# Rotary embedding on one core: the two tables brought in 8 rows of 8 KB instead of 16 of 4 KB, in the place of slabs 4-5, and no early write of zeros

## The chip, the cores and the metric

The kernel runs on one core of a Trainium2 chip. The metric is the device time of one execution in microseconds. A profile comes from one further execution on the same chip: its *span* runs from the first to the last instruction, and its own time lies a little above the span. TensorE is PE, VectorE DVE, ScalarE ACT, GpSimd POOL; SyncE (SP) computes nothing here and issues DMAs. A core has 16 DMA engines, and an issue on SP's or ACT's queue is spread over them.

## The reference

`x` is (16, 512, 1024) in float32, 16 heads of 64; `cos` and `sin` are (512, 32). Each half of a head is rotated by the angle of its position:

```python
x = x.reshape(batch, seq, num_heads, head_dim)
x1, x2 = x[..., :half_dim], x[..., half_dim:]
cos = cos[None, :, None, :]
sin = sin[None, :, None, :]
rotated = np.concatenate([x1 * cos - x2 * sin,
                          x1 * sin + x2 * cos], axis=-1)
```

So 33.55 MB are read and 33.55 MB written; the tables are 64 KB each.

## The kernel before, in words

**Slabs and places.** The 16 batches form four pairs of *slabs*, 8 MB a pair. A pair covers four batches; each of the 128 partitions holds 16 successive positions of it, the first 8 in the even slab, the other 8 in the odd one, so that a slab has 4 MB, 8192 numbers (32 KB) on each partition. There are three *places* in SBUF, each for two slabs (64 KB on each partition). Slabs 0-1 and 6-7 use place 0, slabs 2-3 place 1, slabs 4-5 place 2. A slab is worked on in its own place: the cast to bf16, the products and the cast back to float32 all lie there.

**Order of the DMAs.** Loads and stores of slabs all go through `issue` (line 66), on SP's queue, and keep the order of the program: load 0, load 1, load 2-3 (even partitions, then odd ones), load 4-5 (whole), then store 0-1 in two halves, load 6-7 in two halves, store 2-3, store 4-5 in halves, store 6-7. An instruction of SP that has to wait holds up all issues behind it. A store waits for ACT's last cast of its slabs, load 6-7 for store 0-1 to have left place 0.

**Tables.** A partition needs cos and sin of its own 8 positions: those of the even slabs in `tabs[0]`, of the odd ones in `tabs[1]`. Each table is read in 16 rows (`TP`) of 1024 numbers (`TW`, 4 KB), one row on every 8th partition (`TS`), by ACT's queue (line 91), into a tile that DVE has set to zero before (line 90). DVE casts both to bf16 (`tab1`, line 114). PE then spreads the rows over all 128 partitions: `pick` holds matrices of 0 and 1 (or −1, for the sign of sin in the lower half), made by POOL (lines 103 to 107), and a matmul with such a matrix copies row j to the partitions it belongs to. A row of 4 KB covers 32 positions and so serves two neighbouring partitions; the index `e` (0 or 1) tells which of the two, and two masked matmuls are added in PSUM (line 122), 16 matmuls in all. DVE copies the first result to bf16 (line 129), ACT the second (through line 154).

**The zeros.** A tile `blank` of 1 x 128 is set to zero (line 84), and ACT's queue writes its 512 bytes to the start of the output (line 93) right behind the tables. Store 0-1 later overwrites them.

**The passes.** For each slab ACT casts x to bf16 (into the first half of the slab's own bytes), DVE multiplies it by the sin and cos tables (line 170, two products), adds the two (line 173) with the halves of a head exchanged, and ACT casts the sum back to float32. ACT casts slab s+1 before it casts slab s back. Slab 0 is done in two passes of 4 positions, slab 7 in three (4, 2, 2).

Of the kernel before, what the change touches and what calls it, by code (L numbers as in the profile page):

```python
# [2 lines left out]

# [4 lines left out]


@with_exitstack  # L10
def kernel(
    ctx: ExitStack,
    tc: tile.TileContext,
    x: bass.AP,
    cos: bass.AP,
    sin: bass.AP,
    num_heads: int,
    out: bass.AP,
):
    nc = tc.nc  # L20
    P = nc.NUM_PARTITIONS

    batch, seq, dim = x.shape
    nh = num_heads
    hd = dim // nh
    half = hd // 2
    bf16 = mybir.dt.bfloat16
    f32 = mybir.dt.float32

    nb = 2  # L30
    nslabs = batch // nb
    rpp = nb * seq // P
    W = rpp * dim
    TP = 16
    TS = P // TP
    TW = seq * half // TP

    out_flat = out.rearrange("b s h d -> b s (h d)")

    singles = ctx.enter_context(tc.tile_pool(name="singles", bufs=1))  # L40
    pairs = ctx.enter_context(tc.tile_pool(name="pairs", bufs=3))
    psum = ctx.enter_context(tc.tile_pool(
        name="psum", bufs=1, space=bass.MemoryType.PSUM))


    def view(t, offset, *dims):
        return dataclasses.replace(t, offset=t.offset + offset,
                                   ap=[t.ap[0], *[list(d) for d in dims]])

    places = [pairs.tile([P, 2 * W], f32, tag="pair", name="pair") for _ in range(3)]


    def here(s, n=1):
        return view(places[s // 2 % 3], s % 2 * W, (1, n * W))


    def there(t, s, n=1):  # L60
        return bass.AP(tensor=t.tensor, offset=t.offset + s // 2 * 2 * P * W + s % 2 * W,
                       ap=[[2 * W, P], [1, n * W]])


    def issue(out, in_):
        tc.keep_in_program_order(nc.sync.dma_start(out=out, in_=in_))  # L66


    def load(s, n=1, parts=slice(None)):
        issue(here(s, n)[parts], there(x, s, n)[parts])  # L70


    def store(s, n=1, parts=slice(None)):
        issue(there(out_flat, s, n)[parts], here(s, n)[parts])


    EVEN, ODD = slice(0, P, 2), slice(1, P, 2)


    load(0)  # L80


    blank = singles.tile([1, P], f32, tag="blank")
    nc.vector.memset(blank, 0.0)  # L84


    cos_sb = singles.tile([P, TW], f32, tag="cos_sb")
    sin_sb = singles.tile([P, TW], f32, tag="sin_sb")
    for t, src in ((cos_sb, cos), (sin_sb, sin)):
        nc.vector.memset(t, 0.0)  # L90
        tc.keep_in_program_order(nc.scalar.dma_start(out=t[::TS], in_=bass.AP(
            tensor=src.tensor, offset=src.offset, ap=[[TW, TP], [1, TW]])))
    tc.keep_in_program_order(nc.scalar.dma_start(out=bass.AP(
        tensor=out_flat.tensor, offset=out_flat.offset, ap=[[P, 1], [1, P]]), in_=blank))

    load(1)
    for parts in (EVEN, ODD):
        load(2, 2, parts)
    load(4, 2)


    pick = singles.tile([P, 4 * P], bf16, tag="pick")
    nc.gpsimd.memset(pick, 0.0)  # L103
    for e in range(2):
        for g in range(2):
            part = view(pick, (2 * e + g) * P + e, (2 * TP, P // (2 * TP)), (2, TP))
            nc.gpsimd.affine_select(  # L107
                out=part, in_=part, compare_op=mybir.AluOpType.not_equal,
                fill=1.0 - 2.0 * g, base=0, pattern=[[0, P // (2 * TP)], [-TS, TP]],
                channel_multiplier=1)  # L110

    tab1 = singles.tile([P, 2 * TW], bf16, tag="tab1")
    for i, t in enumerate((cos_sb, sin_sb)):
        nc.vector.tensor_copy(out=view(tab1, i * TW, (1, TW)), in_=t)  # L114

    accs, tabs = [], []
    for h in range(2):
        acc = psum.tile([P, 2 * rpp * hd], f32, tag=f"acc{h}", name="acc")
        for i in range(2):
            for f in range(2):  # L120
                for e in range(2):
                    nc.tensor.matmul(  # L122
                        view(acc, i * rpp * hd + f * half, (hd, rpp), (1, half)),
                        view(pick, (2 * e + i * f) * P, (1, P)),
                        view(tab1, i * TW + (2 * e + h) * rpp * half, (half, rpp), (1, half)),
                        start=e == 0, stop=e == 1)
        accs.append(acc)
        tabs.append(singles.tile([P, 2 * rpp * hd], bf16, tag=f"tab{h}", name="tab"))
    nc.vector.tensor_copy(out=tabs[0], in_=accs[0])  # L129

    passes = []
    for s in range(nslabs):
        r = 0
        for n in {0: (4, 4), nslabs - 1: (4, 2, 2)}.get(s, (rpp,)):
            passes.append((s, r, n))
            r += n


    def halves(u):
        s, r, n = u
        t = here(s).bitcast(bf16)
        return [view(t, (2 * r + i * n) * dim, (1, n * dim)) for i in range(2)]


    def cast(u):
        s, r, n = u
        copy(halves(u)[0], view(here(s), r * dim, (1, n * dim)))  # L150


    def copy(out, in_):
        tc.keep_in_program_order(nc.scalar.copy(out=out, in_=in_))  # L154


    for i, u in enumerate(passes):
        s, r, n = u
        if i == 0:
            cast(u)  # L160
            cast(passes[1])
            copy(tabs[1], accs[1])
            cast(passes[2])
        elif s > 0:
            for v in passes:
                if v[0] == s + 1:
                    cast(v)
        lo, up = halves(u)
        for t, a in ((up, 0), (lo, rpp * hd)):
            nc.vector.tensor_mul(  # L170
                out=t, in0=lo,
                in1=view(tabs[s % 2], a + r * hd, (hd, n), (0, nh), (1, hd)))
        nc.vector.tensor_add(  # L173
            out=up, in0=up, in1=view(lo, half, (hd, n * nh), (-half, 2), (1, half)))

        copy(view(here(s), r * dim, (1, n * dim)), up)
        if s == 1:
            for act in (store, load):
                for parts in (EVEN, ODD):
                    act(0 if act is store else 6, 2, parts)  # L180
        elif s % 2 and r + n == rpp:
            for parts in (EVEN, ODD) if s == 5 else (slice(None),):
                store(s - 1, 2, parts)


# [1 line left out]
_INS = ['x', 'cos', 'sin', 'num_heads']  # L187
_OUTS = [((16, 512, 16, 64), 'float32')]

_NUMBERS = {'num_heads': 16}  # L190


# [26 lines left out]
```

## Time and profile before

| | |
|---|---|
| median of 3 runs | 162.04 us (161.72 to 162.29) |
| the profiled execution | 162.13 us, span 160.3 us |
| read / written over the span | 33.69 MB / 33.55 MB, 419 GB/s |
| casts of 8192 columns on ACT | 7.02 us each, 12 of them |
| products and sums of 8192 columns on DVE | 4.42 us each, 18 of them |
| matmuls (all for the tables) | 16, 3.7 us busy |
| memset of one table tile | 0.91 us |
| cos and sin, from issue to landing | 7.5 and 9.1 us |

A line of the timeline gives the start in us, the length, the engine, the line of the kernel, the operation with output and input, and how many were merged; in brackets the idle time before it and what ended that. "SPq" and "ACTq" are the issues of DMAs on these queues. In a table of windows the columns are the stretch, its length, each engine's busy time with the number of instructions, the granted clock, the busy share of the DMA engines and their rate. DMA packets are recorded one by one with start, duration, bytes and queue, though not with the engine that moved them; q1 is SP's queue and q10 ACT's. A packet counts in the window in which it starts, so that in windows of a few us the share can be read as above 1.

### The profile page before, as it was taken

The numbers are of one execution on the slowest core, as the hardware profiler recorded it, in microseconds if no ns is written. First come the engines' busy times: TensorE is split into PE (matmuls) and PEld (weight loads), VectorE is DVE, ScalarE is ACT, GpSimd is POOL, SyncE is SP. The second block draws the span as 40 slices with busy tenths as digits, with TensorE's granted clock in tenths as the row PEclk, the third lists the DMA queues.
The fourth block names the chain that finished last, engine by engine and source line by source line (L and its number), as shares of the span: only waits on it lengthen the run. The fifth ranks groups of instructions, "written<-read, shape, count | busy, mean of one in ns | idle before, by whom it ended". The sixth has DMA issues, their size and how long they took to land.

```text
span 160.3 us, 195 instructions
## 1 busy us (share of the span) xinstructions
PE 3.7 (2%) x16; PEld 2.2 (1%) x16; DVE 111.2 (69%) x39; ACT 114.0 (71%) x24; POOL 1.6 (1%) x9
## 2 busy tenths in 40 slices
PE   0026000000000000000000000000000000000000
PEld 0013000000000000000000000000000000000000
DVE  4014699999905998999899899919999997000000
ACT  0306959993399999999999995699999969400000
POOL 4000000000000000000000000000000000000000
DMA  7999999699699698998997996996996996996991
GB/s 262 409 409 393 401 515 523 262 523 523 262 523 523 262 523 376 409 523 376 409 523 327 458 523 294 491 523 278 507 507 294 507 507 278 523 491 294 523 474 49
DMA packets 1426, 67.24 MB, mean 419 GB/s; under 512 B 241, under 2 KB 242, under 8 KB 274
## 3 DMA queue, kind: packets, MB, share of 16 engines
q1 hardware_dynamic: 1360, 67.11, 97.6%
q10 hardware_dynamic: 66, 0.13, 0.2%
HBM read 33.69 MB, written 33.55 MB: 419 GB/s over the span
## 4 chain that ended last, share of the span: by engine, by line
DMA 53%; DVE 16%; ACT 10%; issue 4%; ACTq 2%; SPq 1%
DMA pair<-in_x_dram 37%; DMA out_dram<-pair 15%; DVE pair L170 11%; ACT pair L154 10%; DVE pair L173 5%; ACTq L214 1%; SPq L66 1%; ACTq L154 0%
## 5 line engine op out<-in xcount | busy, mean ns | idle before, releaser
L154 ACT CAST pair<-pair 128x8192 bf16<-128x8192 f32 (+5 forms) x22 | 111.8, 5153 | 19.6 <-DMA pair<-in_x_dram 18.2
L170 DVE TENSOR_TENSOR pair<-pair,tab 128x8192 bf16<-128x8192 bf16 (+2 forms) x22 | 71.4, 3259 | 13.2 <-ACT pair L154 12.9
L173 DVE TENSOR_TENSOR pair<-pair 128x8192 bf16<-128x8192 bf16 (+2 forms) x11 | 35.8, 3260 | 0.3
L114 DVE CAST tab<-cos_sb 128x1024 bf16<-128x1024 f32 x1 | 0.7, 694 | 6.6 <-DMA cos_sb<-in_cos_dram 6.6
L154 ACT ACT_TABLE_LOAD x1 | 1.3, 1283 | 4.4 <-issue 4.4
L122 PE MATMUL acc<-tab,pick 128*128 128x256 bf16 x16 | 3.7, 411 | 12.1 <-DVE tab L114 12.1
L122 PEld LDWEIGHTS <-pick 128*128 128x128 bf16 x16 | 2.2, 139 | 13.1 <-issue 10.6
L114 DVE CAST tab<-sin_sb 128x1024 bf16<-128x1024 f32 x1 | 0.7, 695 | 1.9 <-DMA sin_sb<-in_sin_dram 1.9
L129 DVE CAST tab<-acc 128x1024 bf16<-128x1024 f32 x1 | 1.2, 1225 | 1.1 <-PE acc L122 1.1
L90 DVE MEMSET sin_sb<- 128x1024 f32 x1 | 0.9, 912 | 0.2 <-issue 0.2
L90 DVE MEMSET cos_sb<- 128x1024 f32 x1 | 0.9, 912 | 0.2 <-issue 0.2
L154 ACT CAST tab<-acc 128x1024 bf16<-128x1024 f32 x1 | 1.0, 1006 | 0.0
L107 POOL TENSOR_SCALAR_AFFINE_SELECT pick<-pick 128x64 bf16<-128x64 bf16 x4 | 0.9, 260 | 0.1
L84 DVE MEMSET blank<- 1x128 f32 x1 | 0.2, 165 | 0.8 <-PEq L200 0.8
L103 POOL MEMSET pick<- 128x512 bf16 x1 | 0.5, 524 | 0.3 <-POOLq L200 0.3
L200 POOL MEMSET const-bfloat16-1.0<- 128x1 bf16 x1 | 0.1, 101 | 0.0
L200 POOL MEMSET const-uint8-127<- 128x1 uint8 x1 | 0.1, 101 | 0.0
L200 POOL MEMSET const-float32-0.0<- 128x1 f32 x1 | 0.1, 98 | 0.2 <-issue 0.2
L200 POOL MEMSET const-float32-1.0<- 128x1 f32 x1 | 0.1, 98 | 0.0
## 6 DMA issues: line engine op xcount, KB each, us to landing
pair<-in_x_dram SPq DMA_DIRECT2D x2, 4096.0 KB, 17.5
out_dram<-pair SPq DMA_DIRECT2D x6, 22.8
pair<-in_x_dram SPq DMA_DIRECT2D x5, 35.9
cos_sb<-in_cos_dram ACTq DMA_DIRECT2D x1, 64.0 KB, 7.5
sin_sb<-in_sin_dram ACTq DMA_DIRECT2D x1, 64.0 KB, 9.1
out_dram<-blank ACTq DMA_DIRECT2D x1, 0.5 KB
```

Of the source, the lines that this page charges most:

```text
L66: tc.keep_in_program_order(nc.sync.dma_start(out=out, in_=in_))
L90: nc.vector.memset(t, 0.0)
L103: nc.gpsimd.memset(pick, 0.0)
L107: nc.gpsimd.affine_select(out=part, in_=part, compare_op=mybir.AluOpType.not_equal, fill=1.0 - 2.0 * g, base=0, pattern=[[0, P // (2 * TP) ...
L114: nc.vector.tensor_copy(out=view(tab1, i * TW, (1, TW)), in_=t)
L122: nc.tensor.matmul(view(acc, i * rpp * hd + f * half, (hd, rpp), (1, half)), view(pick, (2 * e + i * f) * P, (1, P)), view(tab1, i * TW + ...
L129: nc.vector.tensor_copy(out=tabs[0], in_=accs[0])
L154: tc.keep_in_program_order(nc.scalar.copy(out=out, in_=in_))
L170: nc.vector.tensor_mul(out=t, in0=lo, in1=view(tabs[s % 2], a + r * hd, (hd, n), (0, nh), (1, hd)))
L173: nc.vector.tensor_add(out=up, in0=up, in1=view(lo, half, (hd, n * nh), (-half, 2), (1, half)))
L200: nc = _bacc.Bacc("TRN2", target_bir_lowering=False, num_devices=1)
L214: with _tile.TileContext(nc) as tc:
```

## The change

A table is now read in 8 rows of 8 KB, one on every 16th partition, into the first 16 KB of place 2 (where slabs 4 and 5 will lie), after DVE has set both areas of 2048 columns to zero. The load of slabs 4-5 is put behind the casts of both tables, which read that place, and is split into even and odd partitions. A row now covers 64 positions and serves four neighbouring partitions (`NE` = 4): `pick` has 8 matrices instead of 4, `tab1` twice the columns, and 32 matmuls take the place of 16, four added up for each part of the result. The tile `blank`, its memset and the write of zeros are gone.

```diff
-    TP = 16
+    TP = 8
     TS = P // TP
+    NE = seq // (2 * rpp * TP)
     TW = seq * half // TP
...
-    blank = singles.tile([1, P], f32, tag="blank")
-    nc.vector.memset(blank, 0.0)
-
-
-    cos_sb = singles.tile([P, TW], f32, tag="cos_sb")
-    sin_sb = singles.tile([P, TW], f32, tag="sin_sb")
+    cos_sb = view(here(4), 0, (1, TW))
+    sin_sb = view(here(4), TW, (1, TW))
     for t, src in ((cos_sb, cos), (sin_sb, sin)):
         nc.vector.memset(t, 0.0)
         tc.keep_in_program_order(nc.scalar.dma_start(out=t[::TS], in_=bass.AP(
             tensor=src.tensor, offset=src.offset, ap=[[TW, TP], [1, TW]])))
-    tc.keep_in_program_order(nc.scalar.dma_start(out=bass.AP(
-        tensor=out_flat.tensor, offset=out_flat.offset, ap=[[P, 1], [1, P]]), in_=blank))
 
     load(1)
     for parts in (EVEN, ODD):
         load(2, 2, parts)
-    load(4, 2)
-
-
-    pick = singles.tile([P, 4 * P], bf16, tag="pick")
+
+
+    pick = singles.tile([P, 2 * NE * P], bf16, tag="pick")
     nc.gpsimd.memset(pick, 0.0)
-    for e in range(2):
+    for e in range(NE):
         for g in range(2):
-            part = view(pick, (2 * e + g) * P + e, (2 * TP, P // (2 * TP)), (2, TP))
+            part = view(pick, (2 * e + g) * P + e, (NE * TP, P // (NE * TP)), (NE, TP))
             nc.gpsimd.affine_select(
                 out=part, in_=part, compare_op=mybir.AluOpType.not_equal,
-                fill=1.0 - 2.0 * g, base=0, pattern=[[0, P // (2 * TP)], [-TS, TP]],
+                fill=1.0 - 2.0 * g, base=0, pattern=[[0, P // (NE * TP)], [-TS, TP]],
                 channel_multiplier=1)
 
     tab1 = singles.tile([P, 2 * TW], bf16, tag="tab1")
     for i, t in enumerate((cos_sb, sin_sb)):
         nc.vector.tensor_copy(out=view(tab1, i * TW, (1, TW)), in_=t)
+
+    for parts in (EVEN, ODD):
+        load(4, 2, parts)
...
-                for e in range(2):
+                for e in range(NE):
                     nc.tensor.matmul(
...
-                        start=e == 0, stop=e == 1)
+                        start=e == 0, stop=e == NE - 1)
```

## The prediction

> **What bounds the kernel now.** I read the page's span and busy shares first, then its DMA lines, then three windows, then the waits and SP's own timeline, and last the packet records of the trace.
>
> ```profile
> span 160.3 us, 195 instructions
> ...
> PE 3.7 (2%) x16; PEld 2.2 (1%) x16; DVE 111.2 (69%) x39; ACT 114.0 (71%) x24; POOL 1.6 (1%) x9
> ...
> q1 hardware_dynamic: 1360, 67.11, 97.6%
> q10 hardware_dynamic: 66, 0.13, 0.2%
> ```
>
> No compute engine is above 71%, while SP's queue (q1, all of x and the output) takes 97.6% of 16 DMA engines for the span. The two tables and the write of zeros are q10: 0.2%.
>
> ```profile
> core 0: us, PE busy (x) PEld busy (x) DVE busy (x) ACT busy (x) POOL busy (x), PEclk, DMA share, GB/s
> 1.70:158.20 156.50, 3.73 (x16) 2.16 (x16) 110.52 (x38) 113.97 (x24) 0.50 (x3) 1.00 1.00 430
> 158.20:160.30 2.10, 0.00 (x0) 0.00 (x0) 0.00 (x0) 0.00 (x0) 0.00 (x0) 1.00 0.00 0
> 0.00:1.70 1.70, 0.00 (x0) 0.07 (x1) 0.72 (x2) 0.00 (x0) 1.11 (x7) 1.00 0.00 0
> ```
>
> Between 1.70 and 158.20 us the DMA share is 1.00. The span is therefore 1.7 us of start, 156.5 us of packets on every DMA engine without a hole, and about 2 us of tail. Only what changes the packets of the fullest DMA engine, or leaves one of them without work, can move the end.
>
> The packet records give start, duration, bytes and queue. Linking each packet to the one that begins where it ends gives 16 chains, one for each DMA engine. Each carries 4.20 MB, among them exactly two packets of 4096 B, one of each table; one also has the 512 B of zeros. From these chains:
> - a 64 KB packet takes 2.418 us from 64 us on, so 32 KB cost 1.21 us, on every engine;
> - a 4096 B table packet takes 0.159 us, its semaphore packet 0.009 us, the zeros 0.027 us. Beside them the x packets on the same engine lengthen by 0.29 to 0.64 us in all, median 0.37;
> - the first x packet lengthens by 0.14 to 0.84 us (mean 0.63); the last load packet ahead of the first store, at 58.7 us, by 0.07 to 0.77 (mean 0.36);
> - the engines end between 158.24 and 159.12 us. That spread comes from these lengthenings and from the first packet's start (1.73 to 2.63 us).
>
> ```profile
> 0.73 2.86 SPq L66 DMA_DIRECT2D pair<-in_x_dram  x5
> 56.70 1.16 SPq L66 DMA_DIRECT2D out_dram<-pair  x2
> 72.14 10.31 SPq L66 DMA_DIRECT2D pair<-in_x_dram  x2
> 84.38 53.96 SPq L66 DMA_DIRECT2D out_dram<-pair  x4
> ```
>
> SP's issues run ahead of the packets: the first store is issued at 56.70 us and its packets begin at 61.4; the next store at 84.38, packets at 100.1. Only the last store, issued at 138.0, is just in time: four engines stand still for 0.09 to 0.14 us there. It follows load 6 (landed at 101.3) by 36.7 us of casts, multiplies and copies. So a DMA engine that brings load 6 late also makes the last store late by as much.
>
> **The change part by part.** Durations are those of the profiled execution: 162.13 us with a span of 160.3, 1.8 us lying around it. It stands 0.09 us above the median of 162.04, and I take that off at the end.
>
> *Zeros.* Gone are one memset (0.17 us of DVE, off the path), one issue on ACT's queue (0.68 us at 3.7, ahead of an idle stretch until 13.62) and 0.027 + 0.009 us on one DMA engine: −0.04 us there, nothing elsewhere. Whether the early write made the first store cheaper, no row shows; the bounds are below nothing: −0.04, and above: the first stores cost as much as the first loads, 0.63 − 0.36 = +0.27 us mean, at the worst single packets 0.84 − 0.07 = +0.77. I take nothing, because the first store still pays 0.36 with the zeros written, and the engine that wrote them pays 0.29, hardly less than the rest.
>
> *Eight rows of 8 KB.* The 16 rows of a table went one to an engine, and packets of 32 and 64 KB stay whole, so 8 rows can reach 8 engines at most. If both tables fall on the same eight, these carry 2 × 8 KB in place of 2 × 4 KB: +2 × 0.159 = +0.32 us, with as many interleavings as before (0.37 stays). The other eight lose everything: −(2 × 0.168 + 0.37) = −0.71 us. If the second table takes the other eight, nobody gains bytes and each loses one interleaving: about −0.2. I take the same eight, as nothing in the two issues differs but the source, and what counts is the fullest engine. The one that ends last (159.12) is in the loaded half with even chance, and then the end moves by +0.32. Else it is the last of those that are loaded: by the ends of the chains when load 6 arrives (100.94, 100.77, 100.66, 100.64, 100.63, then 100.41 and earlier) that moves the maximum by +0.15, +0.04, or at best −0.2. Weighted by halves: 0.5 × 0.32 + 0.25 × 0.15 + 0.25 × 0 = +0.20; I take +0.25, since a loaded engine also brings load 6, and with it the last store, late. Bounds −0.5 and +0.32.
>
> [...]
>
> *Memsets and table lateness.* 1024 columns take 0.912 us and 128 take 0.165, so 2048 take 0.912 + 1024 × 0.83 ns = 1.77. The first memset starts where that of the zeros did (0.82) and the table is issued at 2.6 in place of 2.08; the second at 4.5 in place of 3.16. A landing took 7.5 and 9.1 us from issue; with one x packet of 1.21 us more for a missed turn the tables are there by 11.5 and 14.1 at the latest.
>
> ```profile
> 9.72 0.69 DVE L114 CAST tab<-cos_sb 128x1024 bf16<-128x1024 f32 x1 [6.59 <-DMA cos_sb<-in_cos_dram]
> ...
> 12.34 0.69 DVE L114 CAST tab<-sin_sb 128x1024 bf16<-128x1024 f32 x1 [1.93 <-DMA sin_sb<-in_sin_dram]
> ...
> 13.09 2.72 PE L122 MATMUL acc<-tab,pick 128*128 128x256 bf16 x12 [1.61 <-DVE tab L114]
> ...
> 17.26 6.82 DVE L170 TENSOR_TENSOR pair<-pair,tab 128x4096 bf16<-128x4096 bf16 x3 [1.90 <-ACT pair L154]
> ...
> 49.79 8.88 DVE L170 TENSOR_TENSOR pair<-pair,tab 128x8192 bf16<-128x8192 bf16 x2 [5.72 <-ACT pair L154]
> ```
>
> Each cast doubles to 1.39 us, so the second ends at 15.5. A matmul costs 2.72 / 12 = 0.227 us. Eight of the first accumulation are then left: 17.3; the table copy of 1.23 ends at 18.6. The first multiply came at 17.26, so DVE is late by up to 1.3 us. Slabs 0 and 1 run on without a gap, and the lateness ends in the 5.72 us idle before 49.79. ACT needs the second table at 20.64; 16 more matmuls give 20.9, and the 0.3 us go into its 1.68 us idle before 23.33. Cost nothing; beyond 4.3 us of lateness it would push ACT's copy at 49.66 and then the first store. Eight selects of POOL at 0.26 and a memset of about 1.0 end near 4 us, the weights being needed at 10.5.
>
> *Slabs 4-5 loaded late, in two.* SP now stands at this load until the second cast is done, 15.5 us. Behind it is only the first store (56.7). Its packets are needed when slabs 2-3 are through, 42.2 us: 26 us of cover, less 0.5 for the second issue. The two halves move the same bytes, and the load of slabs 2-3, halved already, has the same 1.21 us for 32 KB. One more semaphore packet: 0.009. Nothing.
>
> Sum: 162.13 − 0 + 0.25 + 0 = 162.38, less 0.09: **162.3 us**.
>
> **Rivals.**
>
> *The first store pays for the missing write* (slower). Place: the change from loads to stores near 58.7 us, where all engines lengthen together. For it: the first packets of the loads cost 0.63, of the stores 0.36, and a later change from loads to stores (100.1 us) only 0.02, so first use has a price. Against it: the zeros reached one engine, and it fared no better. Price +0.27 to +0.77 beside the 0.25: 162.6 to 163.1, say 162.8. It decides once the removal costs 0.25 us.
>
> *The unloaded half holds the late engines* (faster). The chains that start last (1.93 to 2.63 us) also end last (158.45 to 159.12), and the four waits before the last store, at 138.9, 139.2, 139.4 and 139.7, are in the same order, as if descriptors were always dealt out in one order. If those are the engines without tables, they come 0.71 earlier and the others (158.24 to 158.37) 0.32 later, near 158.65: 0.47 less at the end, 161.55. Against it: the last store's issue follows load 6, which improves by 0.2 only.
>
> *The table rows crowd each other where they land.* If x rows beside them lengthen twice as much, 0.37 more on the loaded engines: 162.7. Against it: 32 table packets took 0.159 to 0.167 each, and the lengthening hardly varies among engines. [...]
>
> *The tables come over 4.3 us late.* PE's first use or a table issue slips by several x packets; each us beyond the cover costs one: about 164.
>
> *The rows are cut up among 16 engines after all*: then nothing changes but the zeros, 162.0.
>
> **How the numbers follow.** A measurement of this kernel can tell about 0.3%, 0.49 us, from no change. Forecast 0.45 (within 0.33, slower 0.11, faster 0.01; its own range 161.7 to 162.6); missing write 0.23 (slower 0.21, within 0.02); late engines relieved 0.18 (faster 0.15, within 0.03); crowding 0.05 (slower 0.04, within 0.01); late tables 0.03 (slower); cut up 0.06 (within 0.05, faster 0.01). That is faster 0.17, within 0.44, slower 0.39. The range 161.5 to 163.2 leaves out half of the relieved case's better end and the late tables and worst first stores.
>
> **What would show it.** In the packet records: 16 table packets of 8192 B, all in the same eight chains, those chains about 1 us behind the others at 42 us; mean lengthening at the first store near 0.36. In the timeline: load of slabs 4-5 issued between 13 and 16 us, DVE's first multiply between 17.3 and 18.6, idle time left before slab 2's multiplies. In the windows: DMA share still 1.00 to the end. Wrong would be a hole in the DMA share anywhere, or lengthened packets away from the tables.

## The result and the profile after

| | kernel before | changed kernel |
|---|---|---|
| median of 20 runs | 161.91 us (161.62 to 162.29) | 162.40 us (161.90 to 163.13) |
| ratio | | 1.0030, 95% interval 1.0018 to 1.0042 |
| profiled execution, span | 162.13 us, 160.3 us | 162.42 us, 160.6 us |

By the ratio the change costs 0.49 us (0.29 to 0.68). The DMA lines of the changed kernel's page:

```profile
DMA packets 1408, 67.24 MB, mean 419 GB/s; under 512 B 240, under 2 KB 240, under 8 KB 240
...
q1 hardware_dynamic: 1376, 67.11, 97.6%
q10 hardware_dynamic: 32, 0.13, 0.2%
```

The bytes are those of before, 67.24 MB. q10 has 32 packets for 66: 16 rows of 8 KB and 16 semaphores. Besides the semaphores, nothing under 8 KB is left.

Its table of windows, over the same kinds of stretch:

```profile
1.70:158.20 156.50, 5.86 (x32) 4.26 (x32) 113.39 (x38) 113.97 (x24) 1.52 (x8) 0.56 1.00 430
158.20:160.60 2.40, 0.00 (x0) 0.00 (x0) 0.00 (x0) 0.00 (x0) 0.00 (x0) 0.50 0.00 0
0.00:1.70 1.70, 0.00 (x0) 0.00 (x0) 0.47 (x1) 0.00 (x0) 1.15 (x5) 1.00 0.00 0
```

The DMA share between 1.70 and 158.20 us is 1.00 again. In the packet records the first packet starts at 1.74 us (1.73 before), and the last one ends at 159.45 us instead of 159.12, with 1.2 us of span behind it in both: the time lies in the packets. SP's own timeline:

```profile
0.73 16.04 SPq L67 DMA_DIRECT2D pair<-in_x_dram  x6
57.42 1.16 SPq L67 DMA_DIRECT2D out_dram<-pair  x2
72.41 10.27 SPq L67 DMA_DIRECT2D pair<-in_x_dram  x2
85.10 53.74 SPq L67 DMA_DIRECT2D out_dram<-pair  x4
```

The group of loads now ends at 16.77 us instead of 3.59, because SP waits for the table casts (the second ends at 15.63); no other issue stands behind it until 57.42. The stores are issued 0.5 to 0.7 us later than before, the last one at 138.5 instead of 138.0. And the table path, in the timeline of all engines:

```profile
14.40 1.23 DVE L108 CAST tab<-pair 128x2048 bf16<-128x2048 f32 x1 [1.73 <-DMA pair<-in_sin_dram]
...
17.53 1.23 DVE L126 CAST tab<-acc 128x1024 bf16<-128x1024 f32 x1 [1.90 <-PE acc L119]
18.85 6.82 DVE L167 TENSOR_TENSOR pair<-pair,tab 128x4096 bf16<-128x4096 bf16 x3
...
50.51 8.89 DVE L167 TENSOR_TENSOR pair<-pair,tab 128x8192 bf16<-128x8192 bf16 x2 [4.86 <-ACT pair L151]
```

The first multiply comes at 18.85 us instead of 17.26. By slab 2 that is gone: DVE still idles 4.86 us there (5.72 before) and waits for ACT.

ACT's first cast of slab 6 starts when load 6 has landed. In the kernel before:

```profile
101.40 27.97 ACT L154 CAST pair<-pair 128x8192 bf16<-128x8192 f32 x6 [3.20 <-DMA pair<-in_x_dram]
```

and in the changed one, 0.50 us later:

```profile
101.90 27.96 ACT L151 CAST pair<-pair 128x8192 bf16<-128x8192 f32 x6 [2.98 <-DMA pair<-in_x_dram]
```

Where the time went is to be seen in the packet records. "Lengthening" is what an x packet takes beyond the usual 1.213 us for 32 KB or 2.418 us for 64 KB. One chain each (start in us, x for a packet of x, T for one of the tables' queue, its bytes, its duration in us; T4 is a semaphore), from the profiles of before and of the changed kernel:

```
before, a DMA engine (all 16 are like it)
 6.22 x32768 1.219 |  7.43 T4096 0.167 |  7.60 x32768 1.311 |  8.90 T4 0.009
 8.91 x32768 1.364 | 10.27 T4096 0.167 | 10.43 x32768 1.319 | 11.75 T4 0.009 | 11.75 x32768 1.213
changed, one with tables
 6.04 x32768 1.213 |  7.25 T8192 0.309 |  7.55 x32768 1.375 |  8.92 T4 0.009
 8.93 x32768 1.251 | 10.18 T8192 0.318 | 10.49 x32768 1.578 | 12.06 T4 0.009 | 12.07 x32768 1.253
changed, one without
 6.23 x32768 1.213 |  7.44 x32768 1.374 |  8.81 x32768 1.256 | 10.06 x32768 1.572 | 11.63 x32768 1.264
```

Eight chains carry both tables, 2 x 8 KB each, 0.64 us with the semaphores where all 16 spent 0.34. But the x packets of the other eight lengthen just as much, by 0.16 us while cos lands and 0.36 while sin does. Summed up to 20 us, the lengthening of x packets after the first has a median of 0.43 us in this profile of before and 0.65 in that of the changed kernel.

### The profile page after: what moved, and what is told of

It is laid out like the page before. It is cut to its first block, busy times and chain, and to the rows that moved or that the text cites. A ratio compares the mean times of both kernels' runs of the same rounds, so it can differ in the third digit from the quotient of the medians.

```text
span 160.6 us, 236 instructions
## 1 busy us (share of the span) xinstructions
PE 5.9 (4%) x32; PEld 4.3 (3%) x32; DVE 113.9 (71%) x38; ACT 114.0 (71%) x24; POOL 2.7 (2%) x13
## 2 busy tenths in 40 slices
DMA packets 1408, 67.24 MB, mean 419 GB/s; under 512 B 240, under 2 KB 240, under 8 KB 240
## 4 chain that ended last, share of the span: by engine, by line
DMA 53%; DVE 16%; ACT 11%; issue 3%; ACTq 2%; SPq 1%
DMA pair<-in_x_dram 38%; DMA out_dram<-pair 15%; DVE pair L167 11%; ACT pair L151 11%; DVE pair L170 5%; ACTq L211 1%; SPq L67 1%; ACTq L151 0%
## 5 line engine op out<-in xcount | busy, mean ns | idle before, releaser
L108 DVE CAST tab<-pair 128x2048 bf16<-128x2048 f32 x2 | 2.5, 1228 | 8.0 <-DMA pair<-in_cos_dram 6.3
L119 PE MATMUL acc<-tab,pick 128*128 128x256 bf16 x32 | 5.9, 370 | 12.7 <-DVE tab L108 12.7
L87 DVE MEMSET pair<- 128x2048 f32 x2 | 3.5, 1765 | 1.6 <-PEq L197 1.2
L119 PEld LDWEIGHTS <-pick 128*128 128x128 bf16 x32 | 4.3, 133 | 14.0 <-issue 10.6
L101 POOL TENSOR_SCALAR_AFFINE_SELECT pick<-pick 128x32 bf16<-128x32 bf16 x8 | 1.5, 257 | 0.1
L97 POOL MEMSET pick<- 128x1024 bf16 x1 | 1.0, 951 | 0.3 <-POOLq L197 0.3
```

The lines of the kernel that those rows point to most:

```text
L101: nc.gpsimd.affine_select(out=part, in_=part, compare_op=mybir.AluOpType.not_equal, fill=1.0 - 2.0 * g, base=0, pattern=[[0, P // (NE * TP ...
L119: nc.tensor.matmul(view(acc, i * rpp * hd + f * half, (hd, rpp), (1, half)), view(pick, (2 * e + i * f) * P, (1, P)), view(tab1, i * TW + ...
```

## The experiments

Each ratio is to the kernel before, run beside it on the same chip.

**The zeros put back into the changed kernel.**

```diff
+    blank = singles.tile([1, P], f32, tag="blank")
+    nc.vector.memset(blank, 0.0)
...
+    tc.keep_in_program_order(nc.scalar.dma_start(out=bass.AP(
+        tensor=out_flat.tensor, offset=out_flat.offset, ap=[[P, 1], [1, P]]), in_=blank))
     load(1)
```

> The changed kernel with the write of zeros put back (memset of 1 x 128, 512 B to the start of the output on ACT's queue behind the tables). Theory of the uneven rows (8 DMA engines carry all of both tables, +0.3 to +0.5 us): no gain, ratio to before 1.003 still. Theory of the missing write (first store pays for it): ratio back to 1.000 to 1.001.

162.52 us, ratio 1.0037 (1.0021 to 1.0053): no gain.

**The zeros taken out of the kernel before.** The same lines removed there.

> The kernel before without the write of zeros and its memset, nothing else. Uneven rows: 1.000 (0.04 us less on one DMA engine). Missing write: 1.002 to 1.003, with the packets ahead of the first store lengthened by more than the 0.36 us of before.

162.01 us, ratio 1.0007 (0.9995 to 1.0019). The packets ahead of the first store lengthened by a mean of 0.48 us, against 0.36 and 0.01 in two profiles of before. That is what the rival of the missing write expected of the packets, but the time did not follow. So the zeros explain none of the loss that the runs can tell; by the interval they could be worth 0.3 us at most, and putting them back earned nothing.

**16 rows of 4 KB in the changed kernel.**

```diff
-    TP = 8
+    TP = 16
```

> The changed kernel with 16 rows of 4 KB for each table (16 matmuls), still staged in place 2, the load of slabs 4-5 still late and in halves, still no write of zeros. Uneven rows: ratio to before 1.000, every chain of packets with two of 4096 B and load 6 landing near 101.3 us. Staging or late load: 1.003 as in the changed kernel. Missing write: 1.003 too.

161.98 us, ratio 1.0009 (0.9995 to 1.0022). Staging, late load and halves remain, and the median of before is nearly reached: they cost nothing that can be told, 0.36 us at most by the interval. All 16 chains had two packets of 4096 B, with a lengthening of 0.50. With the rows, the 16 matmuls and the shorter table tiles came back too, so this run alone does not show that the loss belongs to the rows, and its interval overlaps that of the changed kernel. The reading of each table twice, below, adds packets and no work for a compute engine.

**The kernel before once more.** No edit.

> The kernel before once more, for a second profile. If the lengthening of load packets at the change from loads to stores (0.36 us mean at 58.7 us, 0.02 at 100.1 in the first profile; in the changed kernel 0.03 and 0.36) belongs to the kernel, it shows at 58.7 us again; if it falls on one or the other change by chance, it may stand elsewhere, with the same end.

161.75 us. The lengthening ahead of the first store was 0.01 us this time and did not stand elsewhere (0.03 at the second change from loads to stores); beside the tables it was 0.64 instead of 0.43. One profile's 0.36 was no property of the kernel.

**The 8 rows on other partitions.** Two kernels, with `TS = 4` and `TS = 1`:

```diff
-    TS = P // TP
+    TS = 4
...
-        tc.keep_in_program_order(nc.scalar.dma_start(out=t[::TS], in_=bass.AP(
+        tc.keep_in_program_order(nc.scalar.dma_start(out=t[:TP * TS:TS], in_=bass.AP(
```

> The changed kernel with the 8 rows of a table on every 4th partition (0 to 28) instead of every 16th. In the changed kernel's packet records x packets lengthen by about 0.17 us near 7.5 and 0.36 near 10.3, on the DMA engines without table packets as well. [...] Theory that the lengthening has nothing to do with the partitions: 0.53 again, 1.003.

> The changed kernel with the 8 rows of a table on partitions 0 to 7, side by side. Crowding: the lengthening grows from 0.53 us to 0.8 to 1.1, ratio to before 1.005 to 1.006. Partitions of no account: 0.53 again, 1.003.

Every 4th partition: 162.26 us, 1.0029 (1.0018 to 1.0040). Side by side: 162.67 us, 1.0060 (1.0047 to 1.0074). The records, again one chain each:

```
every 4th partition, with tables
 7.52 T8192 0.309 |  7.83 x32768 1.213 |  9.04 T4 0.009 |  9.04 x32768 1.213
10.25 T8192 0.309 | 10.56 x32768 1.213 | 11.77 T4 0.009 | 11.77 x32768 1.213
side by side, without tables
 7.41 x32768 1.835 |  9.24 x32768 1.213 | 10.45 x32768 2.084 | 12.53 x32768 1.221
```

So the lengthening hangs on where the rows land: 0.00 us in all for every 4th partition, 1.52 for partitions 0 to 7 (0.8 to 1.1 was expected), on all DMA engines alike. It moves the first loads, as the timelines show; every 4th partition first:

```profile
13.39 7.11 ACT L151 CAST pair<-pair 128x4096 bf16<-128x4096 f32 x2 [6.26 <-DMA pair<-in_x_dram]
...
101.62 7.02 ACT L151 CAST pair<-pair 128x8192 bf16<-128x8192 f32 x1 [3.64 <-DMA pair<-in_x_dram]
```

and side by side:

```profile
15.02 7.11 ACT L151 CAST pair<-pair 128x4096 bf16<-128x4096 f32 x2 [8.27 <-DMA pair<-in_x_dram]
...
102.15 27.97 ACT L151 CAST pair<-pair 128x8192 bf16<-128x8192 f32 x6 [2.55 <-DMA pair<-in_x_dram]
```

The first cast starts when load 0 has landed, the second of each pair of lines when load 6 has. At load 0 the two kernels lie 1.63 us apart, at load 6 only 0.53. The kernel with every 4th partition had lost its lead in between: in its records every load packet ahead of the first store lengthened by 0.87 to 1.15 us (mean with the few before it 1.10). Crowding was to bring the lengthening down to 0.37 us or less and the ratio to 1.002 or below. Half of that held: the lengthening beside the tables went, the time did not.

**Each table read twice**, the second time into the place of slab 5, where nothing reads it; in 8 rows and, with `TP = 16`, in 16.

```diff
+    for i, src in enumerate((cos, sin)):
+        tc.keep_in_program_order(nc.scalar.dma_start(out=view(here(5), i * TW, (1, TW))[::TS], in_=bass.AP(
+            tensor=src.tensor, offset=src.offset, ap=[[TW, TP], [1, TW]])))
     load(1)
```

> The changed kernel with each table read a second time, in the same 8 rows, into the place of slab 5, where nothing reads it: the suspected cost doubled. Uneven rows: the same 8 DMA engines carry 2 x 0.31 us more and all lengthen by 0.4 to 0.5 more, +1.0 to 1.1 us, ratio to before 1.009 to 1.010. If only the lengthening counted: +0.5 us, 1.006.

> As the run before, but in 16 rows of 4 KB: the same bytes, evenly spread. Uneven rows: 2 x 0.16 us and some 0.37 of lengthening on every DMA engine on top of the 16-row kernel (1.0009), +0.7 us, ratio 1.005, clearly under the run before. If rows and engines were of no account and only the bytes counted: the same as the run before.

8 rows: 164.22 us, 1.0158 (1.0133 to 1.0183). 16 rows: 162.44 us, 1.0044 (1.0031 to 1.0058). Against the same kernels with the tables read once (1.0030 and 1.0009), the added bytes cost 0.0128 x 161.76 = 2.1 us in 8 rows and 0.0035 x 161.76 = 0.6 in 16. For 16 rows that is near the 1.005 expected; for 8 rows it is twice what was expected (1.009 to 1.010). In 8 rows the lengthening rose to about 2.0 us, from 0.65 and 0.92 in two profiles of the changed kernel; in 16 rows from 0.50 to 0.85. Of the 2.1 us, 0.6 are the added table packets and some 1.2 the added lengthening, an estimate; the rest is open. The same bytes cost more in 8 rows than in 16, with no matmul, memset or cast added in either. When ACT could begin with slab 6 shows it, 8 rows first:

```profile
103.58 27.97 ACT L155 CAST pair<-pair 128x8192 bf16<-128x8192 f32 x6 [2.52 <-DMA pair<-in_x_dram]
```

and 16 rows:

```profile
101.67 7.02 ACT L155 CAST pair<-pair 128x8192 bf16<-128x8192 f32 x1 [2.59 <-DMA pair<-in_x_dram]
```

**The 16 rows of the kernel before on every 4th partition** (the edit as above).

> The kernel before, its 16 rows of a table on every 4th partition (0 to 60) instead of every 8th. Crowding where the rows land: the x packets beside the tables, lengthened by 0.43 and 0.64 us in two profiles of before, lose that (0.1 or less). If that time is won for good: ratio 0.997. If it comes back ahead of the first store, as 1.1 us did with the 8 rows on every 4th partition: 1.000 or above.

161.88 us, 1.0010 (1.0000 to 1.0020). The ratio is the one expected for time that comes back, but not for that reason: the lengthening stayed, 0.47 us beside the tables and 0.28 ahead of the first store.

**The last store split**, in the kernel before and in the changed one.

```diff
+        elif s == nslabs - 2:
+            store(s)
+        elif s == nslabs - 1:
+            if r + n == rpp:
+                store(s)
         elif s % 2 and r + n == rpp:
```

> The kernel before with the last store (slabs 6-7) split into one of slab 6, issued when that is done, and one of slab 7. Theory that the last store comes just in time: the waits of some 0.1 us before its packets vanish, ratio 0.999. If a packet of 32 KB costs what half a packet of 64 KB does: nothing else changes.

> The changed kernel with the same split. Uneven rows: the DMA engines without tables no longer stand for 0.2 to 0.5 us ahead of the last store and end early, but the 8 loaded ones set the end, so the ratio stays near 1.002 to 1.003. Theory that the change costs its time through the late last store: the ratio falls to 1.000.

1.0004 (0.9991 to 1.0017) and 1.0032 (1.0019 to 1.0045). The waits before the last store (0.09 to 0.14 us on four engines of the kernel before, 0.2 to 0.5 us on those without tables in the changed one) are gone in both profiles, and they cost nothing that can be told in either kernel. No version was faster than the kernel before.

Without these waits the ends of the chains show what sets the end. In the kernel before with the split they lie between 158.03 and 158.78 us. In the changed one the eight chains without tables end between 158.21 and 158.58 us and the eight with tables between 158.84 and 159.26. So the loaded engines end last, 0.48 us after the last one of the kernel before, as was expected (one profile each).

**The changed kernel once more.** No edit.

> The changed kernel once more, for a second profile. Uneven rows and crowding: again 8 chains with 0.67 us of table packets, a lengthening near 0.6 to 0.8 us in all 16, and the landing of slabs 2-3 spread by 0.9 us over the DMA engines (0.4 in before).

161.88 us, just under the lowest of its 20 runs above. Slabs 2-3 landed spread over 0.83 us between the DMA engines (0.94 in the first profile, 0.42 and 0.56 in those of before). The lengthening had a median near 0.92 us, more than the 0.6 to 0.8 expected, though the run was among the shortest: the time of one run does not follow from its lengthening alone.

## Why the prediction was right, and where it was not

**Direction and size.** Forecast 162.3 us and slightly slower, measured 162.40. That the number is so close is in part luck: the forecast change was +0.25 us and the measured one +0.49 (0.29 to 0.68), and the median of before, 161.91 in 20 runs instead of 162.04 in 3, took back 0.13 of that difference. The bound by the DMA engines (share 1.00 from 1.70 to 158.20 us), and the cover for everything else, held. Staging and the late load in halves cost nothing that can be told (1.0009 with 16 rows in the changed kernel). For the longer memsets and casts, the 16 more matmuls and the eight selects no run stands alone, but the profile shows them covered: the 1.3 us by which DVE was to be late at most were 1.59, and DVE still idles 4.86 us ahead of slab 2, where ACT waits for a load. The second cast ended at 15.63 us (15.5 forecast) and the table copy at 18.76 (18.6).

**The zeros: nothing, as taken.** Both runs on them agree. What stood for that rival in the profile, some 0.6 us for the first loads against 0.36 for the first stores, was weak: the 0.36 was 0.01 in the next profile.

**Eight rows on eight engines: +0.32 on the fullest, as taken.** Both tables fell on the same eight chains, and these carried 0.30 us more (0.64 less 0.34). With the last store split they ended last, all eight.

**The step that failed: "The other eight lose everything".** The 0.37 us of lengthening was put down to interleaving on an engine's own queue, to stay on the loaded engines and vanish on the others. It does neither: all 16 lengthen together, and more than before (0.65 and about 0.92 us in two profiles, 0.43 and 0.64 in those of before). The unloaded engines gain some 0.34 us of table packets and give back 0.2 to 0.3. Where slabs 2-3 land, near 42 us, they were to be 0.71 us early and the loaded ones 0.32 late; by the means of two profiles each they were 0.01 early and the loaded ones 0.45 late, so the loaded chains lay 0.49 and 0.43 us behind the others and not about 1 us. The records also have "lengthened packets away from the tables", on the engines without them, which the prediction named as a sign of being wrong. So the relief that was to bring the mean term down from 0.32 to 0.25, and the whole of the faster rival, were not there. Counting the lengthening beside the tables and at the two changes from loads to stores, the two profiles of the changed kernel have 0.65 + 0.04 + 0.35 and 0.92 + 0.01 + 0.02 us, a mean of 1.00, those of before 0.43 + 0.36 + 0.03 and 0.64 + 0.01 + 0.03, a mean of 0.75. The term would have been 0.30 + 0.25 = 0.55 us, an estimate from two profiles each; 0.49 was measured. With so few profiles the agreement proves little.

**Crowding, given 0.05, was a part of the truth.** It was rejected because the lengthening hardly varied among the engines; the runs show that all of them lengthen together, whichever carry the rows (by 0.16 and 0.36 us on the eight without tables too). By where the rows land, the lengthening measured was:

- 8 rows on every 4th partition: 0.00 us
- 16 rows on every 8th: 0.43 to 0.64; on every 4th: 0.47
- 8 rows on every 16th: 0.65 to 0.92 (0.82 to 1.04 with the zeros or the split)
- 8 rows side by side: 1.52

That the placement matters is shown. The spacing alone does not give this order: moved to every 4th partition, the 8 rows lost all of the lengthening, and the 16 rows kept 0.47 us where 0.1 or less was expected. Through what the placement acts, no run shows.

**Late engines relieved, rows cut up, tables too late**: none occurred. The engines without tables were indeed mostly late ones (first packets at a mean of 1.97 us against 1.87, in the second profile 2.08 against 1.80), but the relief of 0.71 us was not there. The late last store was no cause either (1.0032 with it split).

How the 0.49 us divide between the 0.30 and the lengthening stays partly open, since the placement without any lengthening was no faster (last section).

## What to carry to other kernels

With the DMA engines busy throughout (share 1.00), a small side transfer cost here what it did to the fullest engine and to the traffic beside it (by an estimate 0.30 and 0.25 us, where 0.49 was measured): spread it over all 16 engines rather than make its rows longer (1.0009 against 1.0030, read twice 1.0044 against 1.0158), and do not land its rows side by side (1.0060). Among the wider spacings tried no difference in time could be told (1.0029 on every 4th partition, 1.0030 on every 16th). Compute work that doubled stayed covered (DVE came 1.59 us late and still idled 4.86 us); 8 KB more on half of the DMA engines did not (0.30 us more on each, and with the last store split they ended last). A lengthening that is equal on all engines is not evidence against crowding where the rows land (side by side it was 1.52 us on all of them), and one profile's transition costs should be seen in a second profile before they are priced (0.36 us at the first store, then 0.01).

## What the runs showed of the hardware that was not expected

Where table rows landed side by side, x packets of DMA engines without table packets lengthened too: by 0.62 and 0.87 us for one packet each.

Profiles with less lengthening beside the tables had more of it ahead of the first store. The median over the DMA engines of the lengthening beside the tables, and the mean of that ahead of the first store, in us:

| kernel (profile) | tables | first store |
|---|---|---|
| 8 rows, every 4th partition | 0.00 | 1.10 |
| before, first profile | 0.43 | 0.36 |
| before, rows on every 4th partition | 0.47 | 0.28 |
| before without zeros | 0.48 | 0.48 |
| changed, 16 rows | 0.50 | 0.23 |
| before, second profile | 0.64 | 0.01 |
| changed, first profile | 0.65 | 0.04 |
| changed with zeros | 0.82 | 0.01 |
| 8 rows side by side | 1.52 | 0.01 |

The five other profiles fit in: 0.52 and 0.16 in the kernel before with the split, 0.85 to 2.0 and 0.01 in the rest. From 0.64 us on next to nothing is left at the first store. One profile each shows that the two go together, not that the one brings the other about. What the load packets wait for there is not settled: the first store's issue was 1.84 to 2.04 us ahead of the earliest of these packets in the first six rows, whether they lengthened by 0.01 or 1.10, and only 1.46 to 1.54 in the last three, which lost nothing. So a late issue does not explain it, and no experiment separated other causes.

The granted TensorE clock, a mean over the span, was 0.56 to 0.57 in every run of the kernels with 8 rows and 1.00 in the two profiles of before. No time went with it. In the profile of the changed kernel it was 1.00 until 20 us and 0.50 to 0.52 from there on, and no matmul runs after 18.6 us. On the chip of the last four experiments the kernel before had 0.56 in 9 of 25 runs, with a mean of 161.72 us, and 1.00 in the other 16, with 161.86.
